# Where the split weights and the activations lie in SBUF (mod 256), in a float32 layer whose products run one after another on TensorE

## The chip, the cores and the metric

One core of a Trainium2 chip. The metric is the device time of one launch in microseconds (us). The kernel before was run three times: median 1322.18 us, from 1321.62 to 1323.04. Profiles are of one execution each, and "the span" is the time from the first to the last instruction in such a profile.

## The reference, cut to what matters

One layer of a streaming encoder, for 256 tokens of a new stream and 32 tokens of a running one (288 tokens in all), in float32:

```
xn   = rmsnorm(x)                       # 2048 features
proj = xn @ w_in                        # 2048 x 5664: pool input | gate z | conv input | dt
y    = concat[pool_mixer(...), ssd_mixer(...)]      # 3072 features
x    = x + rmsnorm(y @ w_out)           # 3072 x 2048
up   = causal_conv(rmsnorm(x) @ w_up)   # 2048 x 11264
x    = x + rmsnorm((silu(gate) * val) @ w_down)     # 5632 x 2048
```

The outputs are x, the running states and the last rows of each convolution. By far most of the work is the four large products.

## The kernel before, in words

**How a product is made.** Activations lie transposed, features on the 128 partitions and the 288 tokens along the free dimension. A float32 product is put together from three faster ones: each operand is split into a high part (rounded to the type float32r) and a low part (what is left). `mm3` (L143 to L146) issues, for one block of 128 x 128 weights and one tile of tokens, high weights with the tokens' high part (L144), high weights with the tokens' low part (L145) and low weights with the tokens' high part (L146), all into the same accumulator. Each is a weight load and a matmul over 288 columns.

**How a stage runs.** `project` (L148) takes two output tiles of 128 columns at a time. For each it fetches weights in blocks of 8 k-tiles x 256 columns (`fetch_w`, L119, a DMA on SP into a buffer `raw`), splits them in steps of 4 k-tiles (`split_w`, L126: the high part `whi` by ScalarE at L138, the low part `wlo` by VectorE at L139), and issues the three matmuls for each k-tile and output tile. The stages in order: a hand-ordered first stage (L361) with six output tiles and weights of its own, in tiles `w`; then w_in with tokens `xn`; w_out with tokens `mixp` (pool mixer) and `mixs` (SSD mixer); w_up with tokens `hn`; half of w_down with tokens `fa`; w_up again, and the other half of w_down. The last two output tiles are made in another way (L1265, L1266, L1288). The order on every engine comes from a list scheduler with priorities, from `keep_in_program_order` and from `issue_after`.

**Where tiles lie.** A pool gives each of its tags `bufs` slots of the size of the largest tile of that tag, padded to a multiple of 32 bytes per partition; pools lie one behind the other in the order in which they are opened, and a pool opened later may take the room of one that was closed. Before, the order at the low end of SBUF is: `const` (one slot per tile), `wpool` (four slots each for `hi`, `lo` and `raw`, of 4096, 4096 and 8192 bytes), `side` (hp, eps_t, warm and rec, 32 + 32 + 32 + 64 bytes), `apool` (16 slots of 2304 bytes: xn, mixs, hn and others), then the rest. All sizes in `wpool` are multiples of 256, and 2304 is nine times 256, so all slots of such a pool have the same remainder. A tile of tokens holds the high part first and the low part 1152 bytes behind it, which is 128 mod 256. The room FC_GAP behind `fc_stage` (L1079) puts the 23 tiles `fa` at the remainder that `apool` has.

Byte addresses in a partition, mod 256:

| tile | before | after |
|---|---|---|
| high weights whi | 64 | 96 |
| low weights wlo | 64 | 32 |
| raw weights | 64 | 32 |
| tokens xn, mixs, hn, fa, and du: high part | 224 | 224 |
| the same: low part | 96 | 96 |
| mixp of pool groups 2 and 3: high, low part | 224, 96 | 224, 96 |
| mixp of pool groups 1 and 0: high, low part | 96, 224 | 96, 224 |
| weights w of the first stage: both parts | 160 | 160 |

The lines that the change touches: the pools at L85 to L87; `fetch_w`, `split_w`, `first_load` (L210, which uses slots of all three tags for the first stage's raw weights) and the last two output tiles (L1229 to L1243), which all take buffers from `wpool`; and the small tiles hp, eps_t, warm, rec, g_ssd (L377), wq (L545) and the two places that use the tag `trs` (L661, L1198).

Of the kernel before, what the change touches and what calls it, by code (L numbers as in the profile page):

```python
# [8 lines left out]
F32 = mybir.dt.float32  # L9
F32R = mybir.dt.float32r  # L10
# [6 lines left out]
P = 128  # L17
# [8 lines left out]
HEADS = 32  # L26
# [3 lines left out]
NX = D_SSD // P  # L30
# [12 lines left out]
NB = 768  # L43
# [15 lines left out]
def body(  # L59
# [23 lines left out]
    act, dve, pool, pe, sp = nc.scalar, nc.vector, nc.gpsimd, nc.tensor, nc.sync  # L83

    const = ctx.enter_context(tc.tile_pool(name="const", bufs=1))  # L85
    wpool = ctx.enter_context(tc.tile_pool(name="wpool", bufs=4))
    side = ctx.enter_context(tc.tile_pool(name="side", bufs=1))  # L87
    apool = ctx.enter_context(tc.tile_pool(name="apool", bufs=16))
    bpool = ctx.enter_context(tc.tile_pool(name="bpool", bufs=20))
    acc_ps = ctx.enter_context(tc.tile_pool(name="acc_ps", bufs=5, space=PSUM))  # L90
# [9 lines left out]
    def btile(name):  # L100
        return bpool.tile([P, NT], F32, tag="b", name=name)
# [15 lines left out]
    pin = tc.keep_in_program_order  # L117

    def fetch_w(view, kb, nk, c0, nc_):  # L119
        raw = wpool.tile([P, nk, nc_], F32, tag="raw", name="raw")  # L120
        with tc.high_priority(offset=ahead[0]):
            group, c = divmod(c0, 2 * P)
            sp.dma_start(out=raw, in_=view[group, :, kb : kb + nk, c : c + nc_])
        return raw

    def split_w(raw, kb, nk, nc_, after=()):  # L126

        out = []
        step = min(nk, 1024 // nc_)
        for k in range(0, nk, step):  # L130
            n = min(step, nk - k)
            hi = wpool.tile([P, n, nc_], F32R, tag="hi", name="whi")
            lo = wpool.tile([P, n, nc_], F32R, tag="lo", name="wlo")
            with ExitStack() as order:
                order.enter_context(tc.high_priority(offset=ahead[0]))
                for ins in after:
                    order.enter_context(tc.issue_after(ins.ins))
                act.activation(hi, raw[:, k : k + n, :], AF.Copy)  # L138
                dve.tensor_tensor(lo, raw[:, k : k + n, :], hi.bitcast(F32), op=ALU.subtract)  # L139
            out.append([(kb + k + i, hi[:, i, :], lo[:, i, :]) for i in range(n)])  # L140
        return out
# [6 lines left out]
    def project(view, groups, acts, ksplit, before=None, done=None, spare=(), hold=(), behind=None, wait=(), tail=()):  # L148


        n_all = sum(-(-w // P) for _, w in groups)
        accs = [acc_ps.tile([P, NT], F32, tag="acc", name="acc") for m in range(n_all - len(spare))]
        accs.extend(spare)
        k_first, k_last = ksplit[0][0], ksplit[-1][0] + ksplit[-1][1] - 1
        after = before(*ksplit[0]) if before else None
        for i, (kb, n) in enumerate(ksplit):
            raws = [fetch_w(view, kb, n, c0, w) for c0, w in groups]
            nxt = None
            if before and i + 1 < len(ksplit):
                nxt = before(*ksplit[i + 1])  # L160
            m0 = 0
            for raw, (c0, w) in zip(raws, groups):
                parts = split_w(raw, kb, n, w, tuple(wait) + ((after or ()) if m0 else ()) + (hold if i else tail if m0 + w // P == n_all else ()))
                for q, part in enumerate(parts):
                    for m in range(w // P):
                        c = slice(m * P, (m + 1) * P)
                        with ExitStack() as order:
                            if behind and part[-1][0] == k_last and m0 + m > SUMS_AFTER:
                                order.enter_context(tc.issue_after(behind[-1].ins))
                            for k, hi, lo in part:  # L170
                                mm3(accs[m0 + m], hi[:, c], lo[:, c], acts[k], k == k_first, k == k_last)
                        if done and i + 1 == len(ksplit) and q + 1 == len(parts):
                            done(m0 + m, accs[m0 + m])
                m0 += w // P
            after = nxt
        return accs
# [33 lines left out]
    def first_load(i):  # L210

        kb, n = CHUNKS[i]
        raw = wpool.tile([P, n, NB], F32, tag="raw" if n > 1 else ("hi", "lo")[i % 2], name="raw")
        for j, c in enumerate((slice(0, NB),) if i else PIECES):
            pin((sp if i or j == 2 else act).dma_start(out=raw[:, :, c], in_=w_first[:, kb : kb + n, c]))
        raws.append(raw)

    input_load(0, 1)
    first_load(0)
    for i, (k0, k1) in enumerate(zip(INPUT[:-1], INPUT[1:])):  # L220
        input_load(k0, k1, sp if i else act)
        for j in range(2 * i + 1, 2 * i + 3):
            first_load(j)
    w_dt = xin.tile([P, KD, HEADS], F32, name="w_dt")
    pin(sp.dma_start(out=w_dt, in_=w_dt_in))
    first_load(9)
    cols = const.tile([P, sum(n for _, n in COLS)], F32, name="cols")
    pin(sp.dma_start(out=cols, in_=cols_in))
    hp = side.tile([HEADS, 3], F32, name="hp")
    pin(sp.dma_start(out=hp, in_=heads_in))  # L230
    col = {}
    for name, n in COLS:
# [2 lines left out]

    ones = const.tile([P, P], F32, name="ones")
    pool.memset(ones, 1.0)
    eps_t = side.tile([P, 1], F32, name="eps_t")
    pool.memset(eps_t, EPS)
    warm = side.tile([P, 1], F32, name="warm")  # L240
    pin(act.activation(warm, eps_t, AF.Copy))
    ident = const.tile([P, P], F32, name="ident")
    make_identity(nc, ident)
# [1 line left out]
    pool.affine_select(  # L245
        out=tri, in_=ones, pattern=[[1, P]], compare_op=ALU.is_ge, fill=0.0, base=0, channel_multiplier=-1
    )
    rec = side.tile([P, 16], F32, name="rec")
    for t in range(16):
        pool.memset(rec[:, t : t + 1], 1.0 / (t + 1))  # L250
    scan_one = const.tile([HEADS, NT], F32, name="scan_one")
# [122 lines left out]
    pah = const.tile([P, 5 * NXC], F32, name="pah")  # L374
    c0 = 3 * NXC + 3 * KD
    act.activation(pah, cols[:, c0 : c0 + 5 * NXC], AF.Copy, scale=0.5)
    g_ssd = const.tile([P, NX], F32, name="g_ssd")  # L377
    act.activation(g_ssd, col["ssd_norm"], AF.Copy, scale=0.5)
    start.close()

# [161 lines left out]
    follow(pe.matmul(p_[:, NX:], ones[:HEADS, :], hv[:, NX:], start=True, stop=True))  # L542
    dve.tensor_copy(tok, p_tok[:, :, : 2 * HEADS].rearrange("p b (r h) -> p b r h", r=2))
    dve.tensor_copy(tokd, p_tok[:, :, 2 * HEADS :])
    wq = const.tile([P, HEADS], F32, name="wq")  # L545
    for j in range(3):
        dve.tensor_copy(wq[NS * j : NS * (j + 1)], p_tok[P - NS :, 2, 2 * HEADS :])
    dcol = const.tile([P, NX + HEADS], F32, name="dcol")
# [4 lines left out]
    for i in range(4):  # L553
        o = btile("bc")
# [103 lines left out]

    def token_rstd(p_, scale, name):

        o = const.tile([P, 3], F32, tag="trs", bufs=2, name=name)  # L661
        act.activation(o, p_[:, 0:3], AF.Sqrt, bias=eps_t, scale=scale)
        dve.reciprocal(o, o)
        return o
# [369 lines left out]
    late = []  # L1034
# [114 lines left out]
    for m in range(0, KD, 2):  # L1149
        for p_ in project(w_down[:, :, 0:HALF, :], [(m * P, 256)], f[:HALF], [(0, 8), (8, 8), (16, 6)]):  # L1150
            o = btile("part")
# [43 lines left out]
            ))  # L1195

    def factors(src, bias, n, name):
        o = const.tile([P, 2], F32, tag="trs", bufs=2, name=name)[:, :n]  # L1198
        pin(act.activation(o, src, AF.Sqrt, bias=bias, scale=1.0 / D_MODEL))
        pin(dve.reciprocal(o, o))  # L1200
        return o
# [26 lines left out]
    for (kb, n), raw in zip(K22, raws):  # L1228
        for k in range(0, n, 4):  # L1229
            m = min(4, n - k)  # L1230
            if len(parts) < 4:
                hi = wpool.tile([P, m, 256], F32R, tag="hi", name="whi")
                lo = wpool.tile([P, m, 256], F32R, tag="lo", name="wlo")
            else:
                rest = wpool.tile([P, 2, 4, 256], F32R, tag="raw", name="wlast")
                hi, lo = rest[:, 0, :m], rest[:, 1, :m]
            act.activation(hi, raw[:, k : k + m, :], AF.Copy)
            dve.tensor_tensor(lo, raw[:, k : k + m, :], hi.bitcast(F32), op=ALU.subtract)
            parts.append([(kb + k + i, hi[:, i, :], lo[:, i, :]) for i in range(m)])
    late_ = wpool.tile([P, 6 * P], F32, tag="raw", name="late")  # L1240
    ft.append(late_[:, : 4 * P])
    g_row = late_[:, 4 * P :]
    sp.dma_start(out=g_row, in_=norm_ffn_post[:, A * P :].broadcast_to([P, 2 * P]))  # L1243
# [42 lines left out]
    for k, hi, lo in sum(parts, []):  # L1286
        for x in range(2):
            pin(pe.matmul(  # L1288
                p_0, f2[k][:, x, C0], hi, start=k + x == 0, stop=k == HALF - 1 and x == 1, skip_group_check=True
            ))  # L1290
        if k == SUMS_AT:
            other_sums(sq[0], False)
            rf = factors(p_f, eps_t, 2, "rf1")
        if k == TURN_AT:
            turn(A)
            turn(B)
            pin(act.activation(ft_s[P - NS :, 2 * P :], last_s[P - NS :, :], AF.Copy))

            for i, t in enumerate((A, B)):
                pin(pe.matmul(  # L1300
                    p_0[:, i * P : (i + 1) * P], part[t][:, C0], ident, start=False, stop=False, skip_group_check=True
                ))
# [22 lines left out]
    p_y = acc_ps.tile([P, 512], F32, tag="acc", name="py_")  # L1325
    pin(pe.matmul(p_y, ident, xr[0], start=True, stop=False))
    rf = factors(sum_0, bias_0, 1, "rf0")
    diag = fp.tile([P, P], F32, tag="fc", bufs=6, name="diag")
    pin(act.activation(diag, ident, AF.Copy, scale=rf[:, 0:1]))
# [74 lines left out]
```

## Time and profile before

| | us |
|---|---|
| median of three runs | 1322.18 |
| the profiled execution | 1322.35 |
| its span | 1320.6 |
| TensorE busy, matmuls (10043) | 1313.9 |
| TensorE busy, weight loads (10043) | 1302.5 |
| VectorE busy | 894.7 |
| ScalarE busy | 672.5 |
| GpSimd busy | 251.8 |

In the profile's rows PE is TensorE's matmuls and PEld its weight loads; DVE is VectorE, ACT ScalarE, POOL GpSimd and SP the engine that issues most DMAs. A matmul's row shows its start and how long its record lasts, and records overlap: the next matmul starts long before the record of the last one ends. The throughput is therefore read from the distance of the starts, not from the length of a record. In a row of a window stand the window, its length, and for each engine the busy time with the count of records that touch the window; then the granted share of TensorE's clock (1.00 all through), the share of time that the DMA engines worked, and GB/s. In a row of a timeline stand the start, the time, the engine, the line, the operation, out<-in and how many were merged. In a row of groups stand the count, then the busy time, the mean in ns, and the idle time before with what ended it.

### The profile page before, as it was taken

How to read it: one execution, taken by the hardware profiler on the slowest of the kernel's cores; microseconds unless marked ns; L12 is line 12 of the kernel's file. 1: busy time of each engine (PE TensorE's matmuls, PEld its weight loads, DVE VectorE, ACT ScalarE, POOL GpSimd, SP SyncE). 2: the span in 40 equal slices, each digit the busy share in tenths (PEclk: the TensorE clock that was granted, in tenths of full speed). 3: DMA queues.
4: the chain of work that ended last, by engine and by line, in shares of the span. 5: the costliest groups of instructions: out<-in, count | busy, mean ns of one | idle time of the engine just before them, and what ended most of it. 6: DMA issues, size and time to landing. Idle time of an engine off the chain costs nothing.

```text
span 1320.6 us, 25268 instructions
## 1 busy us (share of the span) xinstructions
PE 1313.9 (99%) x10043; PEld 1302.5 (99%) x10043; DVE 894.7 (68%) x1515; ACT 672.5 (51%) x1013; POOL 251.8 (19%) x399
## 2 busy tenths in 40 slices
PE   9999999999999999999999999999999999999998
PEld 9999999999999999999999999999999999999997
DVE  7998988879655588867766744336666666755454
ACT  7557767446543567544444433334444444444442
POOL 2342222222232221211211200001111111201110
PEclk9999999999999999999999999999999999999999
DMA  8578875445566478666445454455544554466763
GB/s 336 190 217 269 290 220 177 156 163 207 199 218 218 141 197 269 197 179 206 164 160 165 160 166 173 157 171 177 175 160 161 174 173 165 160 228 187 212 178 114
DMA packets 110038, 251.75 MB, mean 191 GB/s; under 512 B 64736, under 2 KB 73856, under 8 KB 87392
## 3 DMA queue, kind: packets, MB, share of 16 engines
q1 hardware_dynamic: 103424, 233.22, 54.7%
q0 software_dynamic: 5824, 16.13, 4.1%
q8 instruction: 78, 1.28, 0.4%
q10 hardware_dynamic: 672, 0.80, 0.2%
q14 instruction: 40, 0.33, 0.1%
HBM read 237.11 MB, written 13.00 MB: 189 GB/s over the span
## 4 chain that ended last, share of the span: by engine, by line
PE 96%; DMA 1%; DVE 1%; ACT 1%; issue 0%; SPq 0%; ACTq 0%
PE acc L145 30%; PE acc L144 30%; PE acc L146 30%; DMA raw<-in_w_first 1%; PE py L633 1%; PE acc L1265 0%; DVE w L300 0%; PE acc L1266 0%; PE acc_t L1288 0%; PE acc_x L145 0%; PE acc_x L144 0%; PE acc_x L146 0%; DVE sq L320 0%; PE py L635 0%; PE acc L361 0%; PE acc_x L361 0%
## 5 line engine op out<-in xcount | busy, mean ns | idle before, releaser
L139 DVE TENSOR_TENSOR wlo<-raw,whi 128x1024 fp32r<-128x1024 f32 (+1 forms) x396 | 472.9, 1196 | 311.9 <-ACT whi L138 310.3
L138 ACT ACTIVATE whi<-raw 128x1024 fp32r<-128x1024 f32 (+1 forms) x396 | 408.4, 1033 | 475.8 <-PE acc L145 394.1
L146 PE MATMUL acc<-hn,wlo 128*128 128x288 f32 x1376 | 404.5, 295 | 0.0
L145 PE MATMUL acc<-hn,whi 128*128 128x288 f32 x1376 | 403.6, 294 | 0.0
L144 PE MATMUL acc<-hn,whi 128*128 128x288 f32 x1376 | 402.9, 294 | 0.5 <-ACT hn L1041 0.4
L144 PEld LDWEIGHTS acc<-hn,whi 128*128 128x128 f32 x1376 | 258.8, 189 | 1.4 <-ACT hn L1041 0.8
L145 PEld LDWEIGHTS acc<-hn,whi 128*128 128x128 f32 x1376 | 258.5, 188 | 0.1
L146 PEld LDWEIGHTS acc<-hn,wlo 128*128 128x128 f32 x1376 | 258.3, 188 | 0.0
L146 PE MATMUL acc<-fa,wlo 128*128 128x288 f32 x660 | 194.6, 295 | 0.0
L145 PE MATMUL acc<-fa,whi 128*128 128x288 f32 x660 | 194.2, 294 | 0.0
L144 PE MATMUL acc<-fa,whi 128*128 128x288 f32 x660 | 194.0, 294 | 0.0
L146 PE MATMUL acc<-xn,wlo 128*128 128x288 f32 x608 | 179.5, 296 | 0.0
L144 PE MATMUL acc<-xn,whi 128*128 128x288 f32 x608 | 179.4, 295 | 0.0
L145 PE MATMUL acc<-xn,whi 128*128 128x288 f32 x608 | 178.9, 294 | 0.0
L144 PEld LDWEIGHTS acc<-fa,whi 128*128 128x128 f32 x660 | 124.5, 189 | 0.0
L145 PEld LDWEIGHTS acc<-fa,whi 128*128 128x128 f32 x660 | 124.1, 188 | 0.0
L146 PEld LDWEIGHTS acc<-fa,wlo 128*128 128x128 f32 x660 | 123.9, 188 | 0.0
L1091 POOL COPY fc_stage<-ebuf 128x4 f32<-128x4 f32 x88 | 26.9, 306 | 476.8 <-DVE ebuf L1090 455.4
L144 PEld LDWEIGHTS acc<-xn,whi 128*128 128x128 f32 x608 | 114.6, 189 | 0.7 <-issue 0.5
L145 PEld LDWEIGHTS acc<-xn,whi 128*128 128x128 f32 x608 | 114.3, 188 | 0.0
L146 PEld LDWEIGHTS acc<-xn,wlo 128*128 128x128 f32 x608 | 114.2, 188 | 0.1
L1086 POOL COPY ebuf<-cols 128x2 f32<-128x2 f32 x88 | 74.0, 842 | 108.7 <-DVE fc L1097 61.2
(338 smaller groups left out, 1800.1 us busy)
## 6 DMA issues: line engine op xcount, KB each, us to landing
raw<-in_w_up SPq DMA_DIRECT2D x80, 1024.0 KB, 5.1
raw<-in_w_in SPq DMA_DIRECT2D x38, 1024.0 KB, 5.2
raw<-in_w_down SPq DMA_DIRECT2D x32, 1024.0 KB, 5.0
raw<-in_w_out SPq DMA_DIRECT2D x24, 1024.0 KB, 5.0
raw<-in_w_down SPq DMA_DIRECT2D x16, 768.0 KB, 4.4
raw<-in_w_up SPq DMA_DIRECT2D x14, 512.0 KB, 4.2
gb<-g_d POOLq DMA_DIRECT2D x8, 832.0 KB, 6.3
raw<-in_w_first SPq DMA_DIRECT2D x5, 768.0 KB, 12.8
```

The source lines that it names most:

```text
L138: act.activation(hi, raw[:, k : k + n, :], AF.Copy)
L139: dve.tensor_tensor(lo, raw[:, k : k + n, :], hi.bitcast(F32), op=ALU.subtract)
L144: then(pe.matmul(out, wh, a[:, 0, :], start=start, stop=False))
L145: then(pe.matmul(out, wh, a[:, 1, :], start=False, stop=False))
L146: then(pe.matmul(out, wl, a[:, 0, :], start=False, stop=stop))
L633: ins = pe.matmul(y[c, 0:256], xw[:, 0, f_], m[:, h, 0:256], start=True, stop=False)
L1086: pool.tensor_copy(e[:, 258:260], hist_f[:, :, i])
L1091: pool.tensor_copy(fc_stage[:, :, :, i], e[:, 256:324].rearrange("p (s c) -> p s c", c=34)[:, :, 0:2])
```

## The change

The one pool of weights becomes three (`whi`, `wlo`, `wraw`), of the same slots and sizes. Between the high parts and the low parts lies a pool `side1` with hp, eps_t, rec and the two slots of `trs`: 32 + 32 + 64 + 64 = 192 bytes. Behind the low parts and the raw weights lies a pool `side2` with g_ssd and wq: 64 + 128 = 192 bytes. The tile warm goes to `const`. `const` is shorter by 224 bytes in all, so that high weights start at 34400 instead of 34624, low weights at 50976 instead of 51008, and `apool` starts where it did, at 100320; every tile above stays in its place. Among tiles that stay in `const`, some move by 32 bytes and some by -32 or more. No instruction is added, removed or put elsewhere in the order, and no wait between engines differs.

```diff
     const = ctx.enter_context(tc.tile_pool(name="const", bufs=1))
-    wpool = ctx.enter_context(tc.tile_pool(name="wpool", bufs=4))
-    side = ctx.enter_context(tc.tile_pool(name="side", bufs=1))
+    wpool = {"hi": ctx.enter_context(tc.tile_pool(name="whi", bufs=4))}
+    side1 = ctx.enter_context(tc.tile_pool(name="side1", bufs=1))
+    wpool["lo"] = ctx.enter_context(tc.tile_pool(name="wlo", bufs=4))
+    wpool["raw"] = ctx.enter_context(tc.tile_pool(name="wraw", bufs=4))
+    side2 = ctx.enter_context(tc.tile_pool(name="side2", bufs=1))
     apool = ctx.enter_context(tc.tile_pool(name="apool", bufs=16))
...
-        raw = wpool.tile([P, nk, nc_], F32, tag="raw", name="raw")
+        raw = wpool["raw"].tile([P, nk, nc_], F32, tag="raw", name="raw")
...
-            hi = wpool.tile([P, n, nc_], F32R, tag="hi", name="whi")
-            lo = wpool.tile([P, n, nc_], F32R, tag="lo", name="wlo")
+            hi = wpool["hi"].tile([P, n, nc_], F32R, tag="hi", name="whi")
+            lo = wpool["lo"].tile([P, n, nc_], F32R, tag="lo", name="wlo")
...
-        raw = wpool.tile([P, n, NB], F32, tag="raw" if n > 1 else ("hi", "lo")[i % 2], name="raw")
+        tag = "raw" if n > 1 else ("hi", "lo")[i % 2]
+        raw = wpool[tag].tile([P, n, NB], F32, tag=tag, name="raw")
...
-    hp = side.tile([HEADS, 3], F32, name="hp")
+    hp = side1.tile([HEADS, 3], F32, name="hp")
...
-    eps_t = side.tile([P, 1], F32, name="eps_t")
+    eps_t = side1.tile([P, 1], F32, name="eps_t")
...
-    warm = side.tile([P, 1], F32, name="warm")
+    warm = const.tile([P, 1], F32, name="warm")
...
-    rec = side.tile([P, 16], F32, name="rec")
+    rec = side1.tile([P, 16], F32, name="rec")
...
-    g_ssd = const.tile([P, NX], F32, name="g_ssd")
+    g_ssd = side2.tile([P, NX], F32, name="g_ssd")
...
-    wq = const.tile([P, HEADS], F32, name="wq")
+    wq = side2.tile([P, HEADS], F32, name="wq")
...
-        o = const.tile([P, 3], F32, tag="trs", bufs=2, name=name)
+        o = side1.tile([P, 3], F32, tag="trs", bufs=2, name=name)
...
-        o = const.tile([P, 2], F32, tag="trs", bufs=2, name=name)[:, :n]
+        o = side1.tile([P, 2], F32, tag="trs", bufs=2, name=name)[:, :n]
```

The last two output tiles take `hi`, `lo`, `rest` and `late_` from the same three pools in the same way.

More of the change, by code (lines that the diff above doesn't have):

```diff
@@ L1231, in body @@
             if len(parts) < 4:
-                hi = wpool.tile([P, m, 256], F32R, tag="hi", name="whi")
-                lo = wpool.tile([P, m, 256], F32R, tag="lo", name="wlo")
+                hi = wpool["hi"].tile([P, m, 256], F32R, tag="hi", name="whi")
+                lo = wpool["lo"].tile([P, m, 256], F32R, tag="lo", name="wlo")
             else:
-                rest = wpool.tile([P, 2, 4, 256], F32R, tag="raw", name="wlast")
+                rest = wpool["raw"].tile([P, 2, 4, 256], F32R, tag="raw", name="wlast")
                 hi, lo = rest[:, 0, :m], rest[:, 1, :m]
@@ L1239, in body @@
             parts.append([(kb + k + i, hi[:, i, :], lo[:, i, :]) for i in range(m)])
-    late_ = wpool.tile([P, 6 * P], F32, tag="raw", name="late")
+    late_ = wpool["raw"].tile([P, 6 * P], F32, tag="raw", name="late")
     ft.append(late_[:, : 4 * P])
```

## The prediction, made before the changed kernel ran

> **What bounds the kernel now.** I read the page first: busy shares, then the chain that ended last; then TensorE's own waits; then TensorE and its weight loads in order of time, in four places.
>
> ```profile
> span 1320.6 us, 25268 instructions
> PE 1313.9 (99%) x10043; PEld 1302.5 (99%) x10043; DVE 894.7 (68%) x1515; ACT 672.5 (51%) x1013; POOL 251.8 (19%) x399
> PE acc L145 30%; PE acc L144 30%; PE acc L146 30%; DMA raw<-in_w_first 1%; PE py L633 1%; PE acc L1265 0%; DVE w L300 0%; PE acc L1266 0%; PE acc_t L1288 0%; PE acc_x L145 0%; PE acc_x L144 0%; PE acc_x L146 0%; DVE sq L320 0%; PE py L635 0%; PE acc L361 0%; PE acc_x L361 0%
> ```
>
> ```profile
> PE acc_x L267 <- DVE busy L194: 1.3, 1, 1.3
> PE py__15330 L1330 <- ACT diag L1329: 0.7, 1, 0.7
> PE acc L144 <- ACT hn L1041: 0.4, 1, 0.4
> ```
>
> The reader is to see that 90% of the span is three lines of one helper (L144, L145, L146), and that TensorE waits for other engines for 2.4 us in all. Nothing done on another engine, and no transfer, shortens this kernel by more than a few us. What counts is the distance in time from one matmul's start to the next: the pace. The following window, TensorE, the weight loads and the other engines by stretch, gives it.
>
> ```profile
> 520.00:760.00 240.00, 240.00 (x1822) 240.00 (x1821) 173.20 (x325) 118.71 (x163) 48.97 (x84) 1.00 0.58 178
> 800.00:900.00 100.00, 100.00 (x761) 100.00 (x760) 39.40 (x35) 38.15 (x47) 0.00 (x0) 1.00 0.51 171
> ```
>
> A matmul's record lasts about 0.29 us, so of 761 some 2.2 reach in from before the window: 100 us / 758.8 = 131.8 ns, and 240 us / 1819.8 = 131.9 ns. The first stretch has DVE at 72% and DMA at 0.58, the second DVE at 39% and POOL at nothing; the pace is the same. So traffic of other engines is not what sets it. I take 131.9.
>
> **The change part by part.** The instructions of the five engines, their order, shapes and semaphore waits are the same in both programs; tile numbers and places in SBUF alone differ. So nothing is added, removed or queued elsewhere, and the whole effect is what addresses do to durations.
>
> Which addresses meet? A weight load runs beside the matmul ahead of it, as these rows show (TensorE, then its loads):
>
> ```profile
> 599.85 0.29 PE L144 MATMUL acc<-hn,whi 128*128 128x288 f32 x1
> 599.85 0.19 PEld L145 LDWEIGHTS acc<-hn,whi 128*128 128x128 f32 x1
> 599.98 0.19 PEld L146 LDWEIGHTS acc<-hn,wlo 128*128 128x128 f32 x1
> ```
>
> So while L144 streams the token's high part, the high weights are loaded again for L145; while L145 streams the token's low part (1152 bytes on, 128 mod 256), the low weights come in for L146; while L146 streams the token's high part, the next high weights come in. Call "distance" the weight block's address less the token block's, mod 256; slices of weights step by 512 bytes and tokens by 2304, so it is the same all along. Before, with weights at 64 and tokens at 224: **96, 224, 96**. After, with high parts at 96 and low parts at 32: **128, 192, 128**. Two other sets of distances stand in this trace. Four of the eight mixp tiles (those of the last two pool groups) lie at 96, which gives 224, 96, 224. In the first stage (L361) w lies at 160, which gives 192, 64, 192; the change leaves that stage alone.
>
> Does the distance matter? The rows show it inside one stage, w_out, with the same code a few us apart:
>
> ```profile
> 447.10 0.29 PE L144 MATMUL acc<-mixs,whi 128*128 128x288 f32 x1
> ...
> 453.39 0.29 PE L144 MATMUL acc<-mixs,whi 128*128 128x288 f32 x1
> ...
> 454.97 0.30 PE L144 MATMUL acc<-mixp,whi 128*128 128x288 f32 x1
> ...
> 458.17 0.29 PE L144 MATMUL acc<-mixp,whi 128*128 128x288 f32 x1
> ```
>
> 48 matmuls lie between the first two rows: 6.29 us / 48 = 131.0 ns at 96, 224, 96. The 24 between the next two have their tokens at 96: 3.20 us / 24 = 133.3 ns at 224, 96, 224. The first stage, at 192, 64, 192:
>
> ```profile
> 40.08 3.37 PE L361 MATMUL acc<-xn,w 128*128 128x288 f32 x24
> 43.29 0.43 PE L361 MATMUL acc_x<-xn,w 128*128 128x288 f32 x2
> ```
>
> 3.21 us / 24 = 133.8 ns, to 10 ns of rounding the same as 133.3. And the main stage is not even:
>
> ```profile
> 739.08 0.29 PE L144 MATMUL acc<-hn,whi 128*128 128x288 f32 x1
> 739.47 0.30 PE L144 MATMUL acc<-hn,whi 128*128 128x288 f32 x1
> 739.88 0.29 PE L144 MATMUL acc<-hn,whi 128*128 128x288 f32 x1
> 740.27 0.29 PE L144 MATMUL acc<-hn,whi 128*128 128x288 f32 x1
> 740.66 0.30 PE L144 MATMUL acc<-hn,whi 128*128 128x288 f32 x1
> ```
>
> Three matmuls lie between neighbouring rows: 0.39, 0.41, 0.39, 0.39 us. One triple in three is dearer; with nine matmuls at 9 x 131.9 = 1187 ns and the dear triple about 404, the six others take some 130.5 each.
>
> My reading: a load at distance 192 or 224 is dear, one at 64 or 96 is cheap. Two dear loads of three give 133.3 (both other sets), one of three gives 131.0 to 131.9. If each load has its own price, 2 cheap + 1 dear = 395.7 ns and 1 cheap + 2 dear = 400.0 make cheap 130.5 and dear 134.8. After the change one load of three is at 192, dear; two are at 128, which no row shows. 128 lies 32 from the cheap 96 and 64 from the dear 192, so I count it as cheap. The price of a load at 128 decides all: from above it is bounded by 134.8, from below by what the columns alone take. For that bound, 256 columns in the last product (L1288):
>
> ```profile
> 1306.74 2.52 PE L1288 MATMUL acc_t<-whi,fa 128*128 128x256 f32 x20
> ```
>
> Taking off the 0.28 us that one record outlasts the last start, 2.24 us / 19 = 118 ns; 32 columns more cost 131.9 - 118 = 14 ns, 0.43 ns each, so 288 columns alone would be 124 ns (an estimate from these two rows).
>
> How many matmuls? Counts of L146, one of three lines:
>
> ```profile
> L146 PE MATMUL acc<-hn,wlo 128*128 128x288 f32 x1376 | 404.5, 295 | 0.0
> L146 PE MATMUL acc<-fa,wlo 128*128 128x288 f32 x660 | 194.6, 295 | 0.0
> L146 PE MATMUL acc<-xn,wlo 128*128 128x288 f32 x608 | 179.5, 296 | 0.0
> L146 PE MATMUL acc<-mixs,wlo 128*128 128x288 f32 x256 | 74.2, 293 | 0.0
> L146 PE MATMUL acc<-mixp,wlo 128*128 128x288 f32 x128 | 37.7, 294 | 0.0
> L146 PE MATMUL acc_x<-hn,wlo 128*128 128x288 f32 x32 | 8.9, 295 | 0.0
> ```
>
> (1376 + 660 + 608 + 256 + 64 + 32) x 3 = 8988 are at the changed distances (of the 128 with mixp, half). I take 130.5 for them, the pace of the six calm ones of nine: the stage keeps one dear load of three, but at 192, farther from both cheap ones, and all three distances become multiples of 64. That is 1.4 ns x 8988 = **12.6 us less**. The 192 with tokens at 96 go to 0, 64, 0: at the 133.3 they have or 2.8 better, 0 to 0.5 us; I take 0. The 176 matmuls of the last two tiles: below 0.3 us either way; 0.
>
> What the addresses do elsewhere: the split of the weights on DVE and ACT reads and writes the moved buffers.
>
> ```profile
> L139 DVE TENSOR_TENSOR wlo<-raw,whi 128x1024 fp32r<-128x1024 f32 x373 | 457.2, 1227 | 290.8 <-ACT whi L138 289.2
> 100.00:200.00 100.00, 100.00 (x839) 97.27 (x838) 91.90 (x172) 73.16 (x142) 26.96 (x43) 1.00 0.82 264
> ```
>
> Before, its three operands start at 64 mod 256; after, at 32, 96 and 32. Its price after is not in the trace. Cover: it stands idle 290.8 us for ACT, and TensorE hides it except where DVE is at 92% (100 to 200 us); there 10% on some 40 splits is 5 us of DVE against 8 idle. I take 0 and keep +3 us.
>
> Sum: span 1320.6 - 12.6 = 1308.0; 1.75 us lie around the span of the profiled execution (1322.35), which is 0.17 over the median of 1322.18: **1310 us**.
>
> **The rivals.**
>
> *128 is dear too* (slower). Then all three loads are dear. In this trace two dear of three and the first stage both stop at 133.3, as if that were a ceiling, and the first stage is the one place where all distances are multiples of 64, as they will be. Price: (133.3 - 131.9) x 8988 = 12.6 us, so **1335**. It decides if the load at 128 costs over (395.7 - 134.8) / 2 = 130.5 by the separate prices: that is exactly the price of 96, and so by that sum alone the change would be worth nothing. I go beyond it because the three paces at equal addresses (131.0, 131.9, six of nine at 130.5) say the loads do not add up one by one but fall into a repeating pattern.
>
> *The distance is worth nothing here*: the new set lands within 0.3 ns of the old pace, **1322**. For it: the separate prices just given. Against it: 131.0 against 133.3 within 12 us of one stage. The Trainium skill has a rule for this rival: in "SBUF — State Buffer", section "SBUF: two separate sides", it holds that among the engines only the port pair shared by DVE and GpSimd makes anyone wait, and TensorE never waits; by it the change is worth 0. The 133.3 of the mixp rows does not agree with it.
>
> *Far more than the calm pace*: loads at 128 meet nothing, pace 128 or less: below 1322 - 3.9 x 8988 ns = **1287**. For it: 124 ns for the columns alone. Against it: no stretch of 288 columns in these rows is under 130. In the Trainium skill, "TensorE: Matmul & The Clock Gate", section "Back-to-back issue gap", N / 2.4 + 2.5 gives 122.5 ns for 288 columns; no row here reaches that, and reaching it would be 84 us.
>
> **How the numbers follow.** Forecast (faster, 1298 to 1319): 0.42. 128 dear: 0.36. Nothing: 0.12. Far more: 0.10. A measurement of this kernel tells about 0.2%, 2.6 us, from no change. So faster 0.52, same 0.12, slower 0.36. Range: up to 1337 (the ceiling and some of DVE's 3 us), down to 1290, which leaves out most of the last rival. Both signs are in it; the forecast's own range is 1298 to 1319.
>
> **What would show it.** Right: in the stretch from 800 us on, some 768 matmuls in 100 us instead of 761, the mean of L139 and L138 as before, and TensorE's waits still a few us. Right in mechanism: the four mixp tiles differ from their neighbours still. Wrong: 752 matmuls in 100 us is the ceiling; 761 is no effect; TensorE waiting for wlo in the first 300 us means that the split became dearer.

## The result, and the profile after

The changed kernel takes 1336.80 us (median of four, 1336.21 to 1337.91), the kernel before 1322.60 (median of four). The ratio is 1.0109, with an interval of 1.0092 to 1.0127: 14.2 us slower, where 12 us less were forecast. The profiled execution took 1336.9 us, its span is 1335.2. The three lines L144 to L146 of before are L147 to L149 now.

First the page of the kernel after (busy times and counts), then TensorE's waits (who waited <- for whom: us in total, times, longest), then the split of the weights on VectorE and ScalarE in the view by groups (busy us, mean ns, idle time before):

```profile
span 1335.2 us, 25268 instructions
PE 1326.7 (99%) x10043; PEld 1316.2 (99%) x10043; DVE 895.3 (67%) x1515; ACT 673.8 (50%) x1013; POOL 254.1 (19%) x399
```

```profile
PE acc L365 <- ACT w L300: 2.0, 1, 2.0
PE acc_x L271 <- DVE busy L197: 1.3, 1, 1.3
PE py__15339 L1334 <- ACT diag L1333: 0.7, 1, 0.7
PE acc L147 <- ACT hn L1045: 0.4, 1, 0.4
```

```profile
L142 DVE TENSOR_TENSOR wlo<-raw,whi 128x1024 fp32r<-128x1024 f32 x373 | 457.9, 1229 | 308.9 <-ACT whi L141 306.7
L141 ACT ACTIVATE whi<-raw 128x1024 fp32r<-128x1024 f32 x373 | 394.1, 1058 | 460.8 <-PE acc L148 372.1 <-issue 77.2 <-PE acc_x L148 2.3
```

The reader is to see what did not change. The counts are the same; VectorE's split costs 1229 ns (1227 before) and ScalarE's 1058 ns as before; TensorE waits for 4.4 us in all, 2.0 more than before, at one place in the first stage. The rest of the 14.6 us of span is TensorE's own pace. The view of windows for TensorE alone (window, length, busy time and count of records, clock, DMA share, GB/s), first before, then after:

```profile
220.00:238.00 18.00, 18.00 (x139) 1.00 0.43 132
530.00:760.00 230.00, 230.00 (x1746) 1.00 0.57 176
```

```profile
220.00:238.00 18.00, 18.00 (x141) 1.00 0.40 125
530.00:760.00 230.00, 230.00 (x1713) 1.00 0.55 173
800.00:900.00 100.00, 100.00 (x746) 1.00 0.48 163
```

With the 2.2 records that reach in, 530 to 760 us has 230 us / 1710.8 = 134.4 ns from start to start, before 131.9. But from 220 to 238 us, with the same three lines and the same distances, there are more matmuls than before, not fewer. The pace is not one number. The timeline of TensorE in the kernel after (start, length, line) shows it by the first and the last row of three windows, all in w_in, with tokens `xn`:

```profile
111.73 0.30 PE L147 MATMUL acc<-xn,whi 128*128 128x288 f32 x1
...
123.99 0.30 PE L149 MATMUL acc<-xn,wlo 128*128 128x288 f32 x1
...
219.74 0.29 PE L148 MATMUL acc<-xn,whi 128*128 128x288 f32 x1
...
237.94 0.29 PE L147 MATMUL acc<-xn,whi 128*128 128x288 f32 x1
...
291.76 0.30 PE L148 MATMUL acc<-xn,whi 128*128 128x288 f32 x1
...
309.91 0.29 PE L148 MATMUL acc<-xn,whi 128*128 128x288 f32 x1
```

92 starts in 12.26 us are **133.3 ns**; 140 in 18.20 us are **130.0**; 135 in 18.15 us are **134.4**. Three paces at one set of addresses, each steady through its window. The start times in the trace show what such a pace is made of: the steps from start to start repeat after six matmuls, at 134.4 as 137, 132, 134, 138, 132, 133 ns, at 133.3 as 140, 132, 134, 133, 136, 125, at 130.0 as 131, 131, 131, 126, 131, 130; the 131.9 of before repeats after nine. The last change in this trace comes just behind two matmuls of another kind (L690, a sum over partitions); the rows around it:

```profile
511.67 0.29 PE L148 MATMUL acc<-hn,whi 128*128 128x288 f32 x1
511.80 0.29 PE L149 MATMUL acc<-hn,wlo 128*128 128x288 f32 x1
511.93 0.65 PE L690 MATMUL psum_t<-msum,ones 128*128 128x288 f32 x2
512.21 0.51 PE L147 MATMUL acc<-hn,whi 128*128 128x288 f32 x1
512.55 0.30 PE L148 MATMUL acc<-hn,whi 128*128 128x288 f32 x1
512.68 0.30 PE L149 MATMUL acc<-hn,wlo 128*128 128x288 f32 x1
```

Behind it nothing else runs on TensorE until the last two output tiles: of the 6204 matmuls with `hn` and `fa` (the counts of the three lines), 5916 come from here on, all at 134.4 ns. So (134.4 - 131.9) x 5916 = 14.8 us: the whole loss, within what the windows' rounding allows. From its first to its last start the stretch takes 795.4 us (512.21 to 1307.65), before 780.1 (512.99 to 1293.12). Everything ahead of it together takes 0.8 us less than before: what the earlier stages win at 130.0 and lose at 133.3, 134.4 and the longer wait nearly cancels.

### The profile page after: what moved, and what is told of

The parts are those of the page before. It is cut to its first block, busy times and chain, and to the rows that moved or that the text cites. A ratio compares the mean times of both kernels' runs of the same rounds, so it can differ in the third digit from the quotient of the medians.

```text
span 1335.2 us, 25268 instructions
## 1 busy us (share of the span) xinstructions
PE 1326.7 (99%) x10043; PEld 1316.2 (99%) x10043; DVE 895.3 (67%) x1515; ACT 673.8 (50%) x1013; POOL 254.1 (19%) x399
## 4 chain that ended last, share of the span: by engine, by line
PE 99%; DMA 1%; DVE 0%; ACT 0%; ACTq 0%; issue 0%
PE acc L147 31%; PE acc L149 30%; PE acc L148 30%; PE acc L365 2%; PE acc_x L365 1%; PE py L637 1%; DMA xg<-in_x_g 1%; PE acc L1269 0%; PE acc L1270 0%; PE acc_t L1292 0%; PE acc_x L147 0%; PE acc_x L149 0%; PE acc_x L148 0%; PE py L639 0%; PE pst L978 0%; PE acc L372 0%
## 5 line engine op out<-in xcount | busy, mean ns | idle before, releaser
L147 PE MATMUL acc<-hn,whi 128*128 128x288 f32 x1376 | 409.7, 300 | 0.4 <-ACT hn L1045 0.4
L149 PE MATMUL acc<-hn,wlo 128*128 128x288 f32 x1376 | 407.8, 297 | 0.0
L148 PE MATMUL acc<-hn,whi 128*128 128x288 f32 x1376 | 405.1, 295 | 0.0
L147 PEld LDWEIGHTS acc<-hn,whi 128*128 128x128 f32 x1376 | 259.0, 189 | 0.9 <-ACT hn L1045 0.8
L149 PEld LDWEIGHTS acc<-hn,wlo 128*128 128x128 f32 x1376 | 258.6, 188 | 0.0
L147 PE MATMUL acc<-fa,whi 128*128 128x288 f32 x660 | 197.7, 300 | 0.0
L149 PE MATMUL acc<-fa,wlo 128*128 128x288 f32 x660 | 196.2, 297 | 0.0
L148 PE MATMUL acc<-fa,whi 128*128 128x288 f32 x660 | 194.9, 295 | 0.0
L147 PE MATMUL acc<-xn,whi 128*128 128x288 f32 x608 | 180.1, 296 | 0.0
L149 PE MATMUL acc<-xn,wlo 128*128 128x288 f32 x608 | 178.8, 294 | 0.0
L147 PEld LDWEIGHTS acc<-fa,whi 128*128 128x128 f32 x660 | 124.6, 189 | 0.0
L149 PEld LDWEIGHTS acc<-fa,wlo 128*128 128x128 f32 x660 | 124.1, 188 | 0.0
L147 PEld LDWEIGHTS acc<-xn,whi 128*128 128x128 f32 x608 | 114.4, 188 | 0.7 <-issue 0.5
L149 PEld LDWEIGHTS acc<-xn,wlo 128*128 128x128 f32 x608 | 114.4, 188 | 0.1
```

What stands on the lines that cost most here:

```text
L147: then(pe.matmul(out, wh, a[:, 0, :], start=start, stop=False))
L148: then(pe.matmul(out, wh, a[:, 1, :], start=False, stop=False))
L149: then(pe.matmul(out, wl, a[:, 0, :], start=False, stop=stop))
```

## The experiments

My theory behind the result: at given distances the stream of matmuls and weight loads settles into one of several repeating patterns, each with a pace, keeps it, and changes it where another matmul interrupts the stream. The rival: the pace follows from the distances alone, and what differs by stretch is other traffic. Each kernel below ran beside the kernel before, whose medians were 1322.2 to 1323.0 us; a time that stands without a ratio is of a single execution.

### Interruptions of 49 lengths, in both layouts

A short product whose output nobody uses (a "kick") is put ahead of groups of 96 matmuls, with 32, 34, ... 128 columns in turn. It adds work and changes no other instruction; in the second kernel the same stands in the layout of before. The expectations speak of 58 groups; there were 49 kicks (10092 matmuls against 10043), one of each length.

```diff
+    def kick(n):
+        k_ = aux([P, NT], "kick")
+        pin(pe.matmul(k_[:, :n], ones_r, ones_r[:, :n], start=True, stop=True))
...
+        kick(32 + 2 * (kicks[0] % 49))
+        kicks[0] += 1
```

> The layout of the changed kernel, with one short product (128 weights, 32 to 128 columns, two more each time, then from 32 again; its result is not used) ahead of each of the 58 groups of output tiles of w_up (all but the first) and of w_down's first half. Theory A (patterns): at one set of addresses TensorE can run in several repeating patterns, here 130.0, 133.3 and 134.4 ns a matmul, and what interrupts the stream decides which comes next; the long stretch from 520 us on kept 134.4 because nothing interrupted it. Then the pace differs from group to group, groups at 130.0 among them, and the 58 short products (about 0.1 us each, 6 us) are more than paid for: 1320 to 1335 us. Theory B (prices by address and stage): the distance of each load gives its price, and hn and fa have a dearer one than xn for a reason of their own; then every group stays at 134.4 and the time is 1337 + 6 = 1343 us.

> The same 58 short products in the kernel before. Theory A: the pace of 131.9 ns breaks up into the paces seen in this layout at other places (131.1, 131.9, 132.4 to 132.9), a narrower spread than in the changed layout; 1322 + 6, give or take 5 us. Theory B: 131.9 in every group, 1328 us.

In the changed layout 1325.53 us, so 11 us less than without the 49 extra products; in the layout of before 1329.51, 7 us more. The timeline of the kicks, in the changed layout, then in that of before, where 96 matmuls lie between neighbouring rows:

```profile
929.39 0.21 PE L1121 MATMUL kick<-ones_r 128*128 128x92 f32 x1
...
942.00 0.21 PE L1121 MATMUL kick<-ones_r 128*128 128x94 f32 x1
...
955.01 0.21 PE L1121 MATMUL kick<-ones_r 128*128 128x96 f32 x1
...
968.03 0.21 PE L1121 MATMUL kick<-ones_r 128*128 128x98 f32 x1
...
980.93 0.21 PE L1121 MATMUL kick<-ones_r 128*128 128x100 f32 x1
...
993.53 0.21 PE L1121 MATMUL kick<-ones_r 128*128 128x102 f32 x1
```

```profile
935.56 0.20 PE L1117 MATMUL kick<-ones_r 128*128 128x92 f32 x1
...
948.36 0.21 PE L1117 MATMUL kick<-ones_r 128*128 128x94 f32 x1
...
961.16 0.21 PE L1117 MATMUL kick<-ones_r 128*128 128x96 f32 x1
...
973.95 0.21 PE L1117 MATMUL kick<-ones_r 128*128 128x98 f32 x1
```

In the changed layout the groups take 12.61, 13.01, 13.02, 12.90 and 12.60 us: less some 0.12 for the kick itself, 130.1, 134.3, 134.4, 133.1 and 130.0 ns each. The same pool of instructions, a few columns apart, falls, to 0.2 ns, into the same three paces that the kernel after showed by itself. The rival, by which every group stays at 134.4, is ruled out. In the layout of before these groups take 12.79 or 12.80, 132.0 to 132.1 ns, and behind all 49 kicks the pace lies between 131.9 and 132.2. The expectation that it would break up there did not come true. So interruptions choose the pattern in the changed layout; in the layout of before none of the 49 leads to another. That layout has more than one all the same: the prediction's rows show 131.0 ns in w_out at the same distances, behind products whose tokens lie elsewhere.

### The two halves of the change, each alone

Unwritten pads place the low parts alone (distances 96, 160, 96), or leave high and low parts together at 96 and so move both against the tokens (128, 0, 128). The pads of the first:

```diff
+    const.tile([P, 56], F32, name="pad_c")
...
+    side2.tile([P, 8], F32, name="pad_2")
```

> One part of the change alone: high weights at 64 as before, low weights at 0 (192 behind the high ones), tokens at 224 as before; distances 96, 160, 96. Theory of separate prices (cheap 130.5 at 64 to 128, dear 134.8 at 192 and 224): 160 unknown between the two; 130.5 to 131.9 ns, 1310 to 1322 us. Theory A: the pace depends on the stretch of the kernel; several paces at these distances too, and the total follows from the pattern that stands from 520 us on.

> The other part alone: high and low weights both at 96, tokens at 224; distances 128, 0, 128. If the load at 128 were what became dear (two of three loads), this has the slow pace as well, 134.4 ns and 1337 us or more, unless 0 is far cheaper than 192. Theory A: several paces at these distances, stretch by stretch, and the total follows from the one that stands from 520 us on.

1327.22 and 1324.31 us: 4.6 and 1.7 us over before, together 6 where the whole change costs 14. The windows, first with the low parts moved, then, in two stretches, with both moved against the tokens:

```profile
530.00:760.00 230.00, 230.00 (x1738) 1.00 0.56 174
```

```profile
60.00:100.00 40.00, 40.00 (x307) 1.00 0.69 207
530.00:760.00 230.00, 230.00 (x1742) 1.00 0.56 175
```

132.5 and, from 530 us on, 132.2 ns. With two loads of three at 128, the second is far from the 134.4 of the changed kernel: a load at 128 is not dear by itself, and the prices of the two edits don't add up. This layout has two paces as well: in w_in, from 60 to 100 us, it runs at 40 us / 304.8 = 131.2 ns.

### One interruption

A single kick ahead of the third group of w_up, of 48 columns (which had kept 130.0 among the 49) or of 128 (which had given 134.4), with the 48 also in the layout of before.

```diff
+        if not spare:
+            if kicks[0] == 1:
+                kick(48)
+            kicks[0] += 1
```

> The layout of the changed kernel and one short product alone (48 columns, result not used), ahead of the third group of w_up at about 519 us; 5916 products follow the last odd one in the changed kernel and kept 134.4 ns. Theory A (repeating patterns, set by what interrupts the stream): after it 130.0 ns up to the last two output tiles at about 1300 us, some 5850 x 4.45 ns = 26 us less: 1311 us, faster than before. Theory B (price by address and stage): 1337 us.

> The layout before, with the one short product of 48 columns at the same place. Theory A: in this layout the pace came back to 131.9 after each of 58 short products, so nothing changes: 1322.5 us. If the short product itself helped whatever the layout, some 10 to 25 us less.

> The same with 128 columns in place of 48. Theory A: with 120 to 128 columns the pace went to 133.3 or 134.4 among the many short products, so 133.3 or 134.4 to the end: 1330 to 1337 us. If any interruption at all were enough (the short product gives the queue time to fill, say), 1311 us as with 48 columns.

1336.34 us (ratio 1.0104, 1.0091 to 1.0117) with 48, so no gain; 1322.72 (1.0001, 0.9992 to 1.0010) in the layout of before; 1330.89 with 128. The windows of the changed layout with 48, then with 128:

```profile
800.00:900.00 100.00, 100.00 (x746) 1.00 0.49 165
```

```profile
800.00:900.00 100.00, 100.00 (x752) 1.00 0.50 169
```

48 left the pattern at 134.4 ns, and 128 moved it to 100 us / 749.8 = 133.4, which is the pace of 133.3 to the rounding of such a window. Among the 49 kicks both had ended elsewhere. So a length has no pattern of its own: which pattern follows depends on the length, since 48 and 128 lead to different ones from the same place and pattern, and it seems to depend on the pattern before. The runs that compare one length also differ in the place of the kick, so that the pattern before decides alone is not shown. That is why the first of these expectations failed: it took 130.0 to belong to 48 columns.

### More interruptions in the stages before

The kick of 48 columns also behind each of the eight groups of SSD products and the first product of the state, with `kick(48)` on a line of its own there.

> The layout of the changed kernel with the one short product of 48 columns and nine more of the same size: one behind each of the eight quads of the SSD mixer, whose products of 64 weights interrupt the w_in stage (133.3 to 134.5 ns from 110 to 172, 242 to 256 and 290 to 310 us in the changed kernel, 130.0 elsewhere), and one behind the first state product in w_out. Theory A: 480 + 96 + 150 products come 3.3 ns nearer together if the short products have there the effect that they have in w_up, 2.4 us, less 0.1 us each: 1309 to 1311 us. If what stands just ahead of them matters as well, some go to 133.3 and the sum is within 1 us of the run with one.

1337.17 us (median of six, 1331.26 to 1338.53; ratio 1.0105, 1.0090 to 1.0121). The windows:

```profile
220.00:238.00 18.00, 18.00 (x137) 1.00 0.38 122
292.00:308.00 16.00, 16.00 (x126) 1.00 0.63 210
800.00:900.00 100.00, 100.00 (x746) 1.00 0.49 161
```

The stretch from 220 us, which had the fast pattern in the kernel after (x141), has lost it to the one of 133.3 (x137): a kick can also spoil a good stretch. The stretch from 292 us, which had 134.4 there, went to 130.0 (x126), so some stretches won and others lost, and the gain that was expected did not come. The long stretch stayed at 134.4 in the profiled execution.

### A sequence that was seen to work: 32, then 34 columns

Among the 49, a kick of 32 had turned 134.4 into 133.3, and the next, of 34, that into 130.0. These two alone, ahead of the second and the third group of w_up; and then ten, of 32, 34, ... 50, ahead of the second to the eleventh.

```diff
+        if not spare:
+            if kicks[0] < 2:
+                kick((32, 34)[kicks[0]])
+            kicks[0] += 1
```

```diff
+            if kicks[0] < 10:
+                kick(32 + 2 * kicks[0])
```

> The layout of the changed kernel and the first two of the 58 short products alone: 32 columns ahead of the second group of w_up and 34 ahead of the third. With one of 48 columns the pace stayed at 134.4 ns, with one of 128 it went to 133.3, with the first two of the 58 it went to 133.3 and then to 130.0. Theory A (the pattern that comes next depends on the one before and on the interruption, and then lasts): 130.0 from 525 us on, 5820 x 4.45 ns = 26 us less than the changed kernel: 1311 us, less than the kernel before. If each of the 58 was needed to hold 130.0 (the pattern does not last by itself over 800 us): between 1311 and 1337 us, with the pace changing in the stretch without short products.

> The layout of the changed kernel and the first ten of the 58 short products (32, 34 ... 50 columns) ahead of the second to the eleventh group of w_up. With two, one execution of five took 1329.8 us where the others took 1309 to 1312; if in that one the second short product met another pattern and led to 133.3, eight more give it other chances, and 130.0 was kept by each of 36 to 50 columns. Theory A: 1311 us and 1 us for the eight, and no execution near 1330. If the slow execution was chance in something else, one of some five again.

With two kicks 1310.73 us (median of five), ratio 0.9913 (0.9898 to 0.9928); one of its five executions took 1329.8 and is not in the interval. With ten 1310.72 (1310.20 to 1311.82, all five together), ratio **0.9912 (0.9899 to 0.9926)**: 11.8 us faster than before, 26 faster than the change alone. The timeline around the second of the two kicks, and the window behind it:

```profile
523.71 0.30 PE L149 MATMUL acc<-hn,wlo 128*128 128x288 f32 x1
523.85 0.29 PE L147 MATMUL acc<-hn,whi 128*128 128x288 f32 x1
523.98 0.30 PE L148 MATMUL acc<-hn,whi 128*128 128x288 f32 x1
524.12 0.29 PE L149 MATMUL acc<-hn,wlo 128*128 128x288 f32 x1
524.25 0.18 PE L1121 MATMUL kick<-ones_r 128*128 128x34 f32 x1
524.28 0.38 PE L147 MATMUL acc<-hn,whi 128*128 128x288 f32 x1
524.49 0.29 PE L148 MATMUL acc<-hn,whi 128*128 128x288 f32 x1
524.62 0.29 PE L149 MATMUL acc<-hn,wlo 128*128 128x288 f32 x1
524.75 0.29 PE L147 MATMUL acc<-hn,whi 128*128 128x288 f32 x1
```

```profile
530.00:760.00 230.00, 230.00 (x1771) 1.00 0.57 179
800.00:900.00 100.00, 100.00 (x771) 1.00 0.52 178
```

Ahead of the kick starts lie 0.14, 0.13 and 0.14 us apart, behind it 0.13 and 0.13; the window gives 230 us / 1768.8 = 130.0 ns, for the whole rest of the stretch. Same addresses, same work, one product of 34 columns between. In all three profiled executions that begin with these two kicks (49, two and ten of them) the paces go from 134.4 over 133.3 to 130.0.

### Is it the distance or the address?

All of SBUF from the weights on is moved by 64 bytes, with the distances kept (high parts at 160, low at 96, tokens at 32). And a layout with all three distances at 96, the value that the prediction had called cheap (high parts at 64, low at 192, tokens at 224).

```diff
+    const.tile([P, 16], F32, name="pad_c")
```

> The changed kernel with 64 bytes of room more in the first pool: high weights at 160, low weights at 96, tokens at 32; all distances as in the changed kernel (128, 192, 128), every address 64 higher. If the distance is what counts: the same paces, 130.0, 133.3 and 134.4, in much the same places, and 1337 us if the long stretch starts in the same pattern. If the addresses themselves count: other paces.

> High weights at 64, low weights at 192, tokens at 224: every load at the same distance, 96, 96, 96, the one that the prediction called cheap. Separate prices: 130.5 ns throughout, 1310 us. Theory A: repeating patterns of this layout's own; the two last output tiles, where all loads were at 96 before, ran at 280 ns a pair of 320 and 288 columns, 11 to 12 ns a matmul over the columns' 0.42 ns each as elsewhere, so 131 to 133 ns and 1318 to 1335 us.

Moved by 64 bytes 1328.87 us; all at 96 1338.62. The windows, first moved by 64 bytes, then all at 96:

```profile
220.00:238.00 18.00, 18.00 (x141) 1.00 0.48 156
292.00:308.00 16.00, 16.00 (x121) 1.00 0.57 201
800.00:900.00 100.00, 100.00 (x752) 1.00 0.49 168
```

```profile
530.00:760.00 230.00, 230.00 (x1727) 1.00 0.56 174
```

With the distances kept, the stretches up to the end of w_out at 465 us have the paces of the kernel after (x141 at 220 us and x121 at 292 us, as there); the long one comes out at 133.3 instead of 134.4, another pattern of the same set. Between them lies the first group of w_up, whose paces differ from trace to trace. Three distances of 96 run at 230 us / 1724.8 = 133.3 ns, in w_in as well as here: the value that appears twice in the 131.9 of before is no cheap one.

## Why the prediction was wrong, by its own steps

- **What bounds the kernel, and that only the pace can move**: right. All counts are the same, and the split costs what it did; what VectorE pays for its new operands, kept at up to 3 us, was nothing. TensorE's waits grew by 2.0 us in the first stage, for `w` on ScalarE, which that step had not seen. This wait is no cost of the change: in the layout of before with 49 kicks it is 1.6 us, in the changed layout moved by 64 bytes there is none, so both layouts have it in some profiles.
- **That the distance mod 256 matters**: right. With the distances kept and all addresses moved by 64 bytes the paces up to 465 us stay; with other distances they are others (one execution of each layout tried for this).
- **A price for each load by its distance, and 128 counted as cheap**: not borne out. Distances of 96 only, all "cheap", run at 133.3 where the prices give 130.5; the low parts alone run at 132.5 where they gave 130.5 to 131.9; the halves of the change cost 4.6 and 1.7 us, the whole 14.
- **"I take 130.5 for them, the pace of the six calm ones of nine"**: this is the step that failed. The prices do not give it: two loads at 130.5 and one at 134.8 are 395.8 ns, 131.9 a matmul and no gain, as the prediction itself says under its first rival. It came from the guess that the loads "fall into a repeating pattern" and that the new layout has one, the calm one. There is no single pace to forecast: at the same distances the changed kernel runs at 130.0, 133.3 and 134.4, by what interrupted the stream last and what pattern it had, and its longest stretch had 134.4. The prediction's own 131.0 and 131.9 at equal distances were a sign of more than one pattern.
- **8988 matmuls at one pace**: only 5916 of them decided, those without an interruption from 512.2 us on. They took 134.4 ns. A pace of 130.0, near the 130.5 of the forecast, was there too, in shorter stretches; two short products bring it to the long one, and then the time is 1310.7 us. That this is the forecast's figure is luck: the forecast did not describe that road.
- **The ceiling of 133.3 in the rival "128 is dear too"**: its time, 1335, is close to the 1336.8, but by two errors: 133.3 is no ceiling (134.4 was measured), and the loads at 128 are not dear (132.2 ns with two of three there, 130.0 in parts of the changed kernel).
- **"Nothing" and "far more"**: no run has held a pace under 130.0 ns over these 288 columns. The 122.5 ns are an estimate from a formula of the Trainium skill ("TensorE: Matmul & The Clock Gate", section "Back-to-back issue gap"), which the section gives for the isolated gap and not for a stream with a weight load for each matmul, as here. The best run stayed 7.5 ns above it; none here shows what takes them.

What stays open: what inside the chip makes the patterns, and by which rule a kick of some columns leads from one to another; why the long stretch of the changed kernel began at 134.4 in all of its four executions (to judge by their times) while one of six with more kicks took 1331.3 and one of five with two kicks 1329.8, times that fit a long stretch at 133.3 but that no profile shows. A kick of 48 columns shows that a length that worked elsewhere need not work here. With ten in a row all five executions lie within 1.6 us; five against five are too few to show that ten are safer than two.

## What to carry to other kernels

Where TensorE is the bound, read its pace stretch by stretch from the distance of starts, and look for places where it changes with nothing changed in the code: one placement of weights and tokens can hold several steady paces, 3.4% apart here. A layout is then not judged by one run of it alone; try it with a few cheap interruptions of different lengths ahead of the long stretch before it is dropped, and run it several times. Don't build a price per load out of paces of two layouts: here such prices held in none of the three layouts for which they gave a figure (the change itself, the low parts alone, all at 96).

## What the runs showed of the hardware that was not expected

- A stream of float32r matmuls of 288 columns with a weight load each runs steadily at 130.0, 133.3 or 134.4 ns in one layout, and keeps its pace for 5916 matmuls (0.8 ms) with the clock at 1.00 and the DMA share at 0.55 in one window of it and 0.48 in another.
- A single matmul of 34 columns, which itself takes some 0.1 us, changed that pace from 133.3 to 130.0 ns for the next 5820 matmuls: some 19 us.
- In the layout of before 49 interruptions of 49 lengths all came back to 131.9 to 132.2 ns.
